# A triangular substitution moved to GpSimd, with a fused state update and fixed priorities, in an RWKV-7 scan

## The chip, the cores and the metric

The kernel runs on one core of a Trainium2 chip. It is one launch; the metric is the device time of that launch in microseconds (us), from its start to its end. The engines named are TensorE (PE, with its weight loads listed apart as PEld), VectorE (DVE), ScalarE (ACT), GpSimd (POOL) and SyncE (SP, which here issues DMA transfers). Each engine works through a queue of its own, in order; between queues, semaphores make an instruction wait for another engine's result.

## The reference, cut to what matters

The reference is one layer of a hybrid encoder: 1024 tokens of 1024 features go through three token mixers (an mLSTM, a long convolution by FFT, and a bidirectional RWKV-7 recurrence), which are gated, projected and merged. The change touches the RWKV-7 recurrence alone. It has 16 heads of 64, and runs once forwards and once backwards over the tokens:

```python
def rwkv7_scan(r, w, k, v, kk, a, reverse):
    def step(state, inp):
        r_t, w_t, k_t, v_t, kk_t, a_t = inp
        sa = jnp.einsum('bhij,bhj->bhi', state, -kk_t)
        state = (state * w_t[:, :, None, :] + sa[..., None] * (kk_t * a_t)[:, :, None, :]
                 + v_t[..., None] * k_t[:, :, None, :])
        return state, jnp.einsum('bhij,bhj->bhi', state, r_t)
    ...
    _, ys = lax.scan(step, jnp.zeros((B, H, N, N), jnp.float32), xs, reverse=reverse)
```

## The kernel before, in words

The launch has four stretches. Until about 865 us come the modulation, the mLSTM and the long convolution; then the preparation of the recurrence's first pair of heads; from 929 to about 1984 us the recurrence over 8 head pairs; then the last norms, the merge and the output projection.

The recurrence is computed in chunks of 64 tokens, 16 chunks a pair, both directions in one go. Inside a chunk the tokens depend on one another through a strictly triangular matrix; its inverse is needed for every chunk and is made ahead of the scan, for eight chunks (one half, g = 0 or 1) at a time, by `tphase`. `tphase` multiplies out the blocks (`pq`, PE), copies them (`quad`, `q21`, ACT), transposes them (`Ab`, DVE, L1625), loads an identity into `Tb` by DMA (L1628), and then solves by substitution: 31 steps, each a product `tm = Ab column x Tb row` and an addition `Tb += tm` (L1630 to L1638; DVE, by the helper at L476). That is 62 instructions that depend on one another, with 16 to 136 elements a partition; it is done 16 times (8 pairs, 2 halves). Two transposes of the result follow (`t1`, L1641, printed as tile `t`, and `t2`, L1644, DVE), then two rounds of small products (`pwx`, PE) and copies into `tt` (ACT). The scan of the chunks of that half reads `tt`.

`scan` runs a chain of links in each chunk m: products U (G by SV, PE); copy `us` out of PSUM (DVE, L1769); products SA (`tt` by `us`, PE); two copies of halves of SA into `SV` (DVE L1775 and ACT L1776); products SN (PE); the new state `sn` = (SN + old state) x `pc`, two DVE instructions (L1787, L1788; helper line L476); two copies of halves of `sn` into the next `SV` (DVE L1800, ACT L1801); the next chunk. The chunk's outputs (`outputs`) are products and copies beside the chain. All tiles U, SA, SN of a chunk lie in one PSUM tile `pch`.

What runs beside the chain: `setup` (the matrices G and B of two chunks), `prep` (decays, keys and so on of the next pair: DVE, ACT, PE), `load`, `post` of the pair before, `bonus`, `tphase` of the next half, and the large products with the input weights (`pg`), which `self.fill` hands out evenly. A weight tile for these is loaded by DMA (`wraw`), cast on ACT (`wh`, L333) and its remainder formed on GpSimd (`wl`, L334); `wl` and `wh` have four buffers each.

The order is set in two ways. `rwkv` has a table of 64 steps a pair, four for each chunk: `put(generator, steps)` says at which steps a generator runs on to its next `yield`, and `weave` goes through the table, filling in products. Then a scheduler of the tile framework, which sees everything that the table has emitted, puts each engine's queue in order by when it expects operands to be ready and by priority: `ahead(tc, ..., TP)` raises `tphase` by 400, `tc.high_priority(10 ** 6)` puts an instruction before all that are ready, and `tc.issue_after(x)` puts it behind x. PSUM tile `banks` ("pq", "pgr", "ptv", "pwx") has one buffer, which these four share.

Of the kernel before, what the change touches and what calls it, by code (L numbers as in the profile page):

```python
# [285 lines left out]
class Trunk:  # L286
# [104 lines left out]
    def in_turn(self, calls, ins=None):  # L391

        for f in calls:
            if ins is None:
                ins = f()  # L395
                continue
            with self.tc.issue_after(ins.ins), self.tc.high_priority(10 ** 6):
                ins = f()  # L398
        return ins

# [946 lines left out]
    def rwkv(self, yc_out, pairs=range(8)):  # L1347
        nc, tc, A = self.nc, self.tc, self.A
        with ExitStack() as c2:
# [39 lines left out]
            n = len(pairs)  # L1389
            cx = [dict(p=p, ar={}, al={}, bk={}, pc={}) for p in pairs]  # L1390
# [10 lines left out]
            for i in range(n):  # L1401
                at = {}

                def put(gen, *steps):
                    for s in steps:
                        at.setdefault(s, []).append(gen)
                put(prep1, 0, 0, 1, 2, 3, 4, 4)
                put(self.bonus(cx[i]), 5, 6, 7)
                put(ahead(tc, self.tphase(cx[i], 1), TP), *range(6, 28, 2))
                if i + 1 < n:  # L1410
# [4 lines left out]
                    put(ahead(tc, self.tphase(nx, 0), TP), *range(39, 62, 2))  # L1415
# [181 lines left out]
    def tphase(self, cx, g):  # L1597
# [3 lines left out]
        nc, rp = self.nc, self.rp  # L1601
# [28 lines left out]
        for l in range(31):  # L1630
            n, m = 31 - l, l // 2 + 1
            x = tm[:, 0:n * m].rearrange("p (a b) -> p a b", b=m)
            self.tt(x, Ab[:, l + 1:32, l].unsqueeze(2).broadcast_to([128, n, m]),
                    Tb[:, l, 0:m].unsqueeze(1).broadcast_to([128, n, m]))
            o = Tb[:, l + 1:32, 0:m]
            self.tt(o, o, x, ADD)
            if l % 5 == 4:
                yield  # L1638
        tt = self.tt_t[g]
        t1 = x2("t1").rearrange("p a b -> p (a b)").rearrange("p (v s) -> p v s", s=16)  # L1640
        nc.vector.transpose(t1.rearrange("p v s -> p s v"), Tb.rearrange("p t s -> p s t"))  # L1641
# [98 lines left out]
    def scan(self, cx, nx):  # L1740
# [13 lines left out]
        for m in range(16):  # L1754
# [14 lines left out]
            nc.vector.tensor_copy(us, U)  # L1769
# [5 lines left out]
            nc.vector.tensor_copy(SV[0:64, 0, both], SA[0:64])  # L1775
            nc.scalar.copy(SV[0:64, 1, both], SA[64:128])  # L1776
# [6 lines left out]
            pc = cx["pc"][g][:, :, c:c + 1].broadcast_to([128, 2, 64])  # L1783
            if m == 0:
                self.tt(S1, SN, pc)
            else:
                self.tt(S1, SN, S0, ADD)  # L1787
                self.tt(S1, S1, pc)  # L1788
# [8 lines left out]
            if m < 15:  # L1797

                SV, at = now[2], now[4]
                nc.vector.tensor_copy(SV[0:64, 0, at], S1[0:64])  # L1800
                nc.scalar.copy(SV[0:64, 1, at], S1[64:128])  # L1801
# [114 lines left out]
```

## Time and profile before

| | us |
|---|---|
| median of 3 runs | 2187.23 (2184.51 to 2191.09) |
| the profiled execution | 2200.05 |
| its span, first to last instruction | 2198.3 |
| first `us` copy of the scan, pair 0 | 929.48 |
| first `us` copy of pair 7 | 1884.68 |
| last `us` copy | 1983.3 |
| mean TensorE clock that the throttle granted | 0.956 of full speed |

The profile has one execution, and all durations come from it; the median comes from runs of their own. A row of a timeline reads: start, duration, engine, source line, operation, output <- inputs, partitions x elements a partition, count, and in brackets how long the engine had been idle and for whom. A row of a group reads: line, engine, operation, output <- inputs, forms, count, then busy time and mean duration in ns, then the idle time before it and what ended that. Helpers record under their own lines: L476 is any DVE two-input operation, L395 and L398 are matmuls that are issued in a fixed turn.

### The profile page before, as it was taken

The page shows a single profiled execution, that of the slowest core. Times are in us where ns is not written, and L with a number is a line of the kernel's source. Part 1 is how long each engine was busy: PE and PEld are TensorE (multiplying, and loading weights), DVE is VectorE, ACT ScalarE, POOL GpSimd, SP SyncE. Part 2 cuts the span into 40 slices and gives each one's busy share as a digit, 9 for nine tenths or more (in the row PEclk, how much of TensorE's full clock was granted, in tenths as well). Part 3 has the DMA queues.
Part 4 walks back from the last instruction along what each step waited for, and adds up shares of the span by engine and source line. Part 5 has one row for each costly group of instructions (what it writes and reads, how often), then busy time and mean ns, then how long its engine had stood idle before and what let it go on. Part 6 is the DMA issues. An engine that isn't in the chain of part 4 may idle for free. (4 is left out here: it accounts for less than half of the span.)

```text
span 2198.3 us, 45984 instructions
## 1 busy us (share of the span) xinstructions
PE 1994.0 (91%) x17098; PEld 1509.2 (69%) x17098; DVE 1634.6 (74%) x4754; ACT 1103.2 (50%) x2558; POOL 424.3 (19%) x485
## 2 busy tenths in 40 slices
PE   6999899999989899899989999999898887897998
PEld 4666777787868677666766676666666665675786
DVE  4854999988447947788787888868887888764536
ACT  5557356454242115664665756667466564532221
POOL 2211311122222432311101111111114411010200
PEclk9999999999999999999998999999899998897999
DMA  8211222334465345321322333224143542445623
GB/s 255 70 67 59 78 77 90 112 101 127 143 200 172 119 138 163 124 68 61 130 79 93 117 106 102 92 81 136 52 155 118 187 144 63 159 143 175 196 89 129
DMA packets 169384, 262.19 MB, mean 119 GB/s; under 512 B 17863, under 2 KB 87335, under 8 KB 169160
## 3 DMA queue, kind: packets, MB, share of 16 engines
q1 hardware_dynamic: 169160, 259.25, 36.3%
q8 instruction: 135, 2.21, 0.4%
q14 instruction: 89, 0.73, 0.1%
HBM read 181.06 MB, written 78.12 MB: 118 GB/s over the span
## 5 line engine op out<-in xcount | busy, mean ns | idle before, releaser
L334 POOL TENSOR_TENSOR wl<-wraw,wh 128x256 fp32r<-128x256 f32 x408 | 371.5, 915 | 1488.6 <-ACT wh L333 1464.8
L351 PE MATMUL pg<-hh,wh 128*128 128x512 f32 x1440 | 601.5, 418 | 20.9 <-ACT wh L333 11.8
L352 PE MATMUL pg<-hh,wl 128*128 128x512 f32 x1440 | 594.3, 413 | 16.4 <-POOL wl L334 16.3
L353 PE MATMUL pg<-hl,wh 128*128 128x512 f32 x1440 | 592.4, 412 | 1.9 <-DVE hl L565 1.8
L351 PEld LDWEIGHTS pg<-hh,wh 128*128 128x128 f32 x1440 | 278.7, 194 | 88.9 <-ACT wh L333 15.1
L352 PEld LDWEIGHTS pg<-hh,wl 128*128 128x128 f32 x1440 | 279.3, 194 | 78.0 <-POOL wl L334 22.2
L353 PEld LDWEIGHTS pg<-hl,wh 128*128 128x128 f32 x1440 | 278.1, 193 | 62.0 <-DVE hl L565 2.8
L333 ACT CAST wh<-wraw 128x256 fp32r<-128x256 f32 x408 | 162.7, 404 | 220.6 <-PE pg L353 122.1
L476 DVE TENSOR_TENSOR tm<-Ab,Tb 128x126 f32<-128x126 f32 (+22 forms) x496 | 145.4, 293 | 4.4 <-DMA Tb<-in_tinit 2.7
L476 DVE TENSOR_TENSOR Tb<-Tb,tm 128x126 f32<-128x126 f32 (+22 forms) x496 | 144.2, 291 | 1.9
L473 DVE SCALAR_TENSOR_TENSOR st<-pg,hmu,st 128x511 f32<-128x511 f32 (+1 forms) x130 | 80.9, 636 | 27.9 <-ACT e L424 17.6
L476 DVE TENSOR_TENSOR G<-pgr,gmask 128x512 f32<-128x512 f32 x128 | 85.4, 679 | 17.0 <-PE pgr L398 17.0
L457 ACT ACTIVATE st<-pg 128x512 f32<-128x512 f32 x74 | 44.2, 597 | 99.9 <-PE pg L353 95.0
L1684 ACT COPY G<-ar 64x128 f32<-64x128 f32 x256 | 64.3, 295 | 48.4 <-DVE G L476 46.6
L473 DVE SCALAR_TENSOR_TENSOR st<-st,pg 128x512 f32<-128x512 f32 x80 | 54.3, 679 | 35.7 <-PE pg L353 12.7
L398 PE MATMUL pgr<-ar,bk 64*128 64x128 f32 x896 | 76.9, 287 | 0.0
L141 DVE SCALAR_TENSOR_TENSOR row<-row 64x1 f32<-64x1 f32 x393 | 72.7, 208 | 2.1
L1769 DVE COPY us<-pch 128x128 f32<-128x128 f32 x128 | 36.3, 283 | 45.8 <-PE pch L398 45.5
L395 PEld LDWEIGHTS pch<-SV,G 128*64 128x64 f32 x256 | 25.3, 139 | 65.5 <-ACT SV L1801 52.3
L395 PE MATMUL pch<-SV,G 128*64 128x64 f32 x256 | 43.2, 252 | 27.7 <-ACT SV L1801 26.2
L476 DVE TENSOR_TENSOR dw<-dw,dw 128x512 f32<-128x512 f32 x92 | 67.1, 760 | 0.9
L395 PEld LDWEIGHTS pch<-SV,B 128*64 128x64 f32 x256 | 25.3, 139 | 60.1 <-ACT SV L1776 50.1
(677 smaller groups left out, 4228.4 us busy)
## 6 DMA issues: line engine op xcount, KB each, us to landing
wraw<-in_w_in SPq DMA_DIRECT2D x340, 128.0 KB, 2.3
low<-lora SPq DMA_DIRECT2D x32, 512.0 KB, 4.1
sig<-st SPq DMA_DIRECT2D x48, 256.0 KB, 2.6
st<-sig SPq DMA_DIRECT2D x48, 256.0 KB, 3.5
wraw<-in_w_br SPq DMA_DIRECT2D x68, 128.0 KB, 2.8
adw<-in_ada_w SPq DMA_DIRECT2D x16, 512.0 KB, 7.1
x<-in_x SPq DMA_DIRECT2D x8, 512.0 KB, 6.1
hx<-st SPq DMA_DIRECT2D x16, 256.0 KB, 2.0
```

Of the source, the lines that this page charges most:

```text
L141: self.ops.append(lambda: self.nc.vector.scalar_tensor_tensor(o, a, s, b, op0=op0, op1=op1))
L333: self.nc.scalar.copy(hi, raw)
L334: self.nc.gpsimd.tensor_tensor(lo, raw, hi.bitcast(F32), op=SUB)
L351: nc.tensor.matmul(p, wh, hh, start=(k == 0), stop=False)
L352: nc.tensor.matmul(p, wl, hh, start=False, stop=False)
L353: nc.tensor.matmul(p, wh, hl, start=False, stop=(k == n - 1))
L395: ins = f()
L398: ins = f()
L457: self.nc.scalar.activation(o, p, AF.Tanh, scale=0.5)
L473: return self.nc.vector.scalar_tensor_tensor(out, in0, s, in1, op0=op0, op1=op1)
L476: return self.nc.vector.tensor_tensor(out, a, b, op=op)
L1684: nc.scalar.copy(G[0:64, :, d, h, 0:64], cx["al"][g, d, b % 4][hsl[h]])
```

## The change

Three things change. The 62 instructions of a substitution are issued on GpSimd instead of DVE; the table gives `tphase` other steps, with one more `yield` ahead of the transposes, and transpose `t1` is to be issued behind the latest `us` copy that has been emitted (`self.mark`). The state update for m > 0 becomes one multiply-add from PSUM for each direction, `sn` = SN x `pc` + `sd`, where `sd` is the old state times `pc`, which ACT has made a chunk ahead. And `us`, the copies into `SV` and `sn` get the highest priority (`first`).

```diff
--- before.py
+++ after.py
@@ -397,6 +397,10 @@
             with self.tc.issue_after(ins.ins), self.tc.high_priority(10 ** 6):
                 ins = f()
         return ins
+
+    def first(self):
+
+        return self.tc.high_priority(10 ** 6)
 
     def banks(self, name):
 
@@ -1387,6 +1391,7 @@
 
             pairs = list(pairs)
             n = len(pairs)
+            self.mark = None
             cx = [dict(p=p, ar={}, al={}, bk={}, pc={}) for p in pairs]
             run(self.load(cx[0]))
             for g in range(2):
@@ -1406,13 +1411,13 @@
                         at.setdefault(s, []).append(gen)
                 put(prep1, 0, 0, 1, 2, 3, 4, 4)
                 put(self.bonus(cx[i]), 5, 6, 7)
-                put(ahead(tc, self.tphase(cx[i], 1), TP), *range(6, 28, 2))
+                put(ahead(tc, self.tphase(cx[i], 1), TP), 6, *range(7, 14), 24, 26, 28)
                 if i + 1 < n:
                     nx = cx[i + 1]
                     put(self.load(nx, cx[i - 1] if i else None), 8, 9, 10, 11)
                     put(ahead(tc, self.prep(nx, 0, 0), PP), 15, 16, 19, 33, 33)
                     put(ahead(tc, self.prep(nx, 0, 1), PP), 34, 35, 36, 37, 37)
-                    put(ahead(tc, self.tphase(nx, 0), TP), *range(39, 62, 2))
+                    put(ahead(tc, self.tphase(nx, 0), TP), 39, *range(40, 47), 57, 59, 61)
                     prep1 = ahead(tc, chain(self.prep(nx, 1, 0), self.prep(nx, 1, 1)), PP)
                     put(prep1, 40, 42, 49)
                 if i > 0:
@@ -1598,7 +1603,7 @@
 
 
 
-        nc, rp = self.nc, self.rp
+        nc, tc, rp = self.nc, self.tc, self.rp
         x2 = lambda n: self.ep.tile([128, 16, 32], F32, name=n, tag="x2", bufs=3)
         q, q21 = x2("quad"), self.ep.tile([128, 16, 32], F32, name="q21", tag="q21", bufs=1)
         pq = [x.rearrange("p (c t) -> p c t", t=CL) for x in self.banks("pq")]
@@ -1630,15 +1635,18 @@
         for l in range(31):
             n, m = 31 - l, l // 2 + 1
             x = tm[:, 0:n * m].rearrange("p (a b) -> p a b", b=m)
-            self.tt(x, Ab[:, l + 1:32, l].unsqueeze(2).broadcast_to([128, n, m]),
-                    Tb[:, l, 0:m].unsqueeze(1).broadcast_to([128, n, m]))
+            nc.gpsimd.tensor_tensor(x, Ab[:, l + 1:32, l].unsqueeze(2).broadcast_to([128, n, m]),
+                                    Tb[:, l, 0:m].unsqueeze(1).broadcast_to([128, n, m]), op=MUL)
             o = Tb[:, l + 1:32, 0:m]
-            self.tt(o, o, x, ADD)
+            nc.gpsimd.tensor_tensor(o, o, x, op=ADD)
             if l % 5 == 4:
                 yield
+        yield
         tt = self.tt_t[g]
         t1 = x2("t1").rearrange("p a b -> p (a b)").rearrange("p (v s) -> p v s", s=16)
-        nc.vector.transpose(t1.rearrange("p v s -> p s v"), Tb.rearrange("p t s -> p s t"))
+
+        with tc.issue_after(self.mark.ins) if self.mark else ExitStack():
+            nc.vector.transpose(t1.rearrange("p v s -> p s v"), Tb.rearrange("p t s -> p s t"))
         t1 = t1.rearrange("p (g u) s -> p u s g", g=2)
         t2 = x2("t2")
         nc.vector.transpose(t2.rearrange("p u (s g) -> p u s g", g=2), t1)
@@ -1766,26 +1774,35 @@
             if late:
                 late[0](ins)
             us = self.sm.tile([128, 2, CL], F32, name="us", tag="us", bufs=2)
-            nc.vector.tensor_copy(us, U)
+            with self.first():
+                self.mark = nc.vector.tensor_copy(us, U)
             ins = self.in_turn(partial(nc.tensor.matmul, SA[hsl[h], d], tt[hsl[h], 8 * d + c, :], us[hsl[h], d],
                                        start=True, stop=True) for d in range(2) for h in range(2))
             if late:
                 late[1](ins)
             late = None
-            nc.vector.tensor_copy(SV[0:64, 0, both], SA[0:64])
-            nc.scalar.copy(SV[0:64, 1, both], SA[64:128])
+            with self.first():
+                nc.vector.tensor_copy(SV[0:64, 0, both], SA[0:64])
+                nc.scalar.copy(SV[0:64, 1, both], SA[64:128])
             yield
             next(ahead, None)
             yield
             self.in_turn(partial(nc.tensor.matmul, SN[hsl[h], d], B[:, j, d, hsl[h]], SV[:, h, at[d]],
                                  start=True, stop=True) for d in range(2) for h in (1, 0))
             S1 = self.sm.tile([128, 2, 64], F32, name="sn", tag="sn", bufs=3)
-            pc = cx["pc"][g][:, :, c:c + 1].broadcast_to([128, 2, 64])
-            if m == 0:
-                self.tt(S1, SN, pc)
-            else:
-                self.tt(S1, SN, S0, ADD)
-                self.tt(S1, S1, pc)
+            pc = cx["pc"][g][:, :, c:c + 1]
+            with self.first():
+                if m == 0:
+                    self.tt(S1, SN, pc.broadcast_to([128, 2, 64]))
+                else:
+                    for d in range(2):
+                        self.stt(S1[:, d], SN[:, d], pc[:, d], S0d[:, d])
+            if m < 15:
+
+                S0d = rp.tile([128, 2, 64], F32, name="sd", tag="sd", bufs=2)
+                pc = cx["pc"][(m + 1) // 8][:, :, (m + 1) % 8:(m + 1) % 8 + 1]
+                for d in range(2):
+                    nc.scalar.activation(S0d[:, d], S1[:, d], AF.Copy, scale=pc[:, d])
             late = self.outputs(y, py, m, S0, ar, now)
             S0 = S1
             if m < 15:
@@ -1797,8 +1814,9 @@
             if m < 15:
 
                 SV, at = now[2], now[4]
-                nc.vector.tensor_copy(SV[0:64, 0, at], S1[0:64])
-                nc.scalar.copy(SV[0:64, 1, at], S1[64:128])
+                with self.first():
+                    nc.vector.tensor_copy(SV[0:64, 0, at], S1[0:64])
+                    nc.scalar.copy(SV[0:64, 1, at], S1[64:128])
             yield
             next(ahead, None)
             yield
```

The first place is DVE's queue where the substitution for the fourth `tphase` ends. `Tb`, `tm`, `Ab` are the substitution, `bk`, `ar`, `P`, `s`, `st` work of `prep` and of the weight products, `us`, `SV`, `sn` links of the chain; `t_` and a number is `t1` or `t2`. Before:

```order
L476 TENSOR_TENSOR Tb<-Tb,tm 128x3x15
L476 TENSOR_TENSOR ar<-r,P 128x4x64
L476 TENSOR_TENSOR tm<-Ab,Tb 128x30
L476 TENSOR_TENSOR bk<-tmp,s 128x4x64
L476 TENSOR_TENSOR Tb<-Tb,tm 128x2x15
L1769 COPY us<-pch 128x128
L476 TENSOR_TENSOR tm<-Ab,Tb 128x16
L476 TENSOR_TENSOR bk<-a,s 128x4x64
L476 TENSOR_TENSOR Tb<-Tb,tm 128x16
L1641 STREAM_TRANSPOSE t_11650<-Tb 128x16x32
```

After, with the line numbers of the changed file (`us` is L1778 there, `SV` L1785 and L1818, `t1` L1649, `t2` L1652):

```order
L477 SCALAR_TENSOR_TENSOR P<-P,hlgb,tmp 128x512
L477 SCALAR_TENSOR_TENSOR s<-s,hlgb,a 128x512
L477 SCALAR_TENSOR_TENSOR sn<-pch,pc,sd 128x64 x2
L477 SCALAR_TENSOR_TENSOR st<-st,pg 128x512
L1818 COPY SV<-sn 64x2x64
L477 SCALAR_TENSOR_TENSOR P<-P,hlgb,tmp 128x512
L1778 COPY us<-pch 128x128
L1649 STREAM_TRANSPOSE t_11757<-Tb 128x16x32
L1785 COPY SV<-pch 64x2x64
L1652 STREAM_TRANSPOSE t_11759<-t_11757 128x512
L477 SCALAR_TENSOR_TENSOR s<-s,hlgb,a 128x512
L480 TENSOR_TENSOR P<-P,tmp 128x512
```

The substitution is gone from this queue. `t1` stands directly behind a `us` copy, and the `SV` copy of the same chunk directly behind `t1`.

The second place is GpSimd's queue, first before, from the weights' remainders of one pair to the next:

```order
L334 TENSOR_TENSOR wl<-wraw,wh 128x256 x14
L1555 MEMSET s 128x8
L334 TENSOR_TENSOR wl<-wraw,wh 128x256 x3
L1555 MEMSET s 128x8 x2
L334 TENSOR_TENSOR wl<-wraw,wh 128x256
L1555 MEMSET s 128x8
L334 TENSOR_TENSOR wl<-wraw,wh 128x256 x3
L1699 MEMSET SV 64x512
```

After, at the end of one substitution and the beginning of the next (L1638 is the product, L1641 the addition, L1560 and L1707 are the memsets that were L1555 and L1699):

```order
L1641 TENSOR_TENSOR Tb<-Tb,tm 128x2x15
L1638 TENSOR_TENSOR tm<-Ab,Tb 128x16
L1641 TENSOR_TENSOR Tb<-Tb,tm 128x16
L334 TENSOR_TENSOR wl<-wraw,wh 128x256 x4
L1560 MEMSET s 128x8
L334 TENSOR_TENSOR wl<-wraw,wh 128x256
L1560 MEMSET s 128x8
L334 TENSOR_TENSOR wl<-wraw,wh 128x256 x2
L1560 MEMSET s 128x8
L1707 MEMSET SV 64x512
L1638 TENSOR_TENSOR tm<-Ab,Tb 128x31
L1641 TENSOR_TENSOR Tb<-Tb,tm 128x31
```

Between two substitutions stand the remainders `wl` and memsets; within a substitution each instruction waits for the one ahead of it, and one to four `wl` are interspersed.

## The prediction

> **What bounds the kernel now.** The share of busy time comes first, then the waits, then windows, since the scan's eight head pairs have stages with different limits.
>
> ```profile
> PE 1994.0 (91%) x17098; PEld 1509.2 (69%) x17098; DVE 1634.6 (74%) x4754; ACT 1103.2 (50%) x2558; POOL 424.3 (19%) x485
> ...
> 929.48 0.29 DVE L1769 COPY us<-pch 128x128 f32<-128x128 f32 x1 [2.31 <-PE pch L398]
> ...
> 1884.68 0.29 DVE L1769 COPY us<-pch 128x128 f32<-128x128 f32 x1 [1.71 <-PE pch L398]
> ```
>
> These are each engine's busy time, and the first copy `us` of pair 0 and of pair 7 (start, length, wait before it in brackets). Seven pairs take 955.2 us, 136.46 us a pair, 8.5 us for each of 16 chunks. PE's 91% has modelled ends, so it is no proof that PE sets the pace. The waits between 929 and 1984 us (total, times, longest) show that the scan's own links are waited for:
>
> ```profile
> POOL wl L334 <- ACT wh L333: 753.2, 132, 39.2
> ACT SV L1801 <- DVE sn L476: 55.4, 39, 4.9
> PEld pch L395 <- ACT SV L1801: 52.3, 71, 5.8
> PEld pch L395 <- ACT SV L1776: 49.6, 81, 2.2
> ACT SV L1776 <- DVE SV L1775: 48.7, 44, 3.9
> DVE us L1769 <- PE pch L398: 45.5, 45, 3.5
> ```
>
> GpSimd idles most, for weights that ACT casts. PE and ACT wait for links that pass through DVE. Where DVE makes them late, windows of pair 2 show (start:end, length, busy time of PE, PEld, DVE, ACT, POOL with instructions, granted clock, DMA share, GB/s):
>
> ```profile
> 1193.34:1207.59 14.25, 12.97 (x235) 9.90 (x237) 10.12 (x20) 11.88 (x29) 1.46 (x2) 1.00 0.34 113
> 1207.59:1246.36 38.77, 35.04 (x322) 25.44 (x318) 35.21 (x115) 23.77 (x60) 6.33 (x8) 1.00 0.41 135
> 1246.36:1270.97 24.61, 23.59 (x465) 17.75 (x464) 19.13 (x41) 21.68 (x52) 1.89 (x4) 1.00 0.30 91
> 1270.97:1306.53 35.56, 33.95 (x333) 24.15 (x331) 32.88 (x127) 16.37 (x42) 6.02 (x8) 1.00 0.20 64
> 1306.53:1323.29 16.76, 16.55 (x241) 12.22 (x243) 8.20 (x20) 11.35 (x22) 0.73 (x1) 1.00 0.43 152
> ```
>
> The second and fourth are the substitutions, from the end of transpose `Ab` to transpose `t1`. There DVE is busy for 35.21 of 38.77 and 32.88 of 35.56 us, 92%: it is full. Elsewhere it is busy for 37.45 of 55.62 us, 67%. The same two windows with `tm` and `Tb` alone (DVE):
>
> ```profile
> 1207.59:1246.36 38.77, 17.46 (x62) 1.00 0.41 135
> 1270.97:1306.53 35.56, 16.64 (x62) 1.00 0.20 64
> ```
>
> So 17.05 us of DVE per substitution, half of its work there, leaves it; 17.0 us stay (17.75 and 16.24). Fifteen such windows lie in the scan. The ends of the first and the last:
>
> ```profile
> 944.07 1.95 DVE L1625 STREAM_TRANSPOSE Ab<-quad 128x1024 f32<-128x1024 f32 x1 [0.39 <-ACT quad L1620]
> 977.89 1.09 DVE L1641 STREAM_TRANSPOSE t<-Tb 128x512 f32<-128x512 f32 x1
> ...
> 1895.73 1.98 DVE L1625 STREAM_TRANSPOSE Ab<-quad 128x1024 f32<-128x1024 f32 x1
> 1937.46 1.10 DVE L1641 STREAM_TRANSPOSE t<-Tb 128x512 f32<-128x512 f32 x1
> ```
>
> The first is 977.89 − 946.02 = 31.9 us, the last 39.8. The 14 of pairs 0 to 6 sum to 541.5, 38.7 each. A pair is thus 2 × 38.7 = 77.4 us of windows and 59.1 us of the rest.
>
> **The substitution on GpSimd.** No row shows `tm` or `Tb` on GpSimd, so T, one substitution there, is built from what it did run:
>
> ```profile
> 198.12 0.73 POOL L334 TENSOR_TENSOR wl<-wraw,wh 128x256 fp32r<-128x256 f32 x1 [1.06 <-DVE row L141]
> 198.87 0.95 POOL L671 MEMSET rm<- 64x1024 f32 x1
> 199.88 0.11 POOL L672 MEMSET rm<- 64x8 f32 x1
> ...
> L930 POOL TENSOR_TENSOR dml<-dw,dmh x4: 1276/1283/1287, 516.7 to 520.4; 128x512 fp32r<-128x512 f32 x4
> ```
>
> A two-input instruction takes 0.73 us for 256 elements a partition and 1.283 for 512: 2.16 ns an element, 0.177 us fixed. Between two GpSimd instructions in a row lie 199.88 − 199.82 = 0.06 us. In step l the loop handles (31 − l)(l // 2 + 1) elements, 2856 in all, twice (multiply and add). T alone = 62 × (0.177 + 0.06) + 2 × 2856 × 0.00216 = 14.7 + 12.3 = 27.0 us.
>
> The Trainium skill, GPSIMD Engine Reference, section "3. Performance versus the Vector engine", measures a GpSimd tensor_tensor at 1.96 times the Vector engine's; 1.96 × 17.05 would make T 33.4 where the sum here comes to 35.6, a total some 33 us lower. The rows agree only roughly: 1.283 us for 512 elements stands beside DVE's 0.68 (1.9 times).
>
> To 27.0 come two things. First, the engines block each other:
>
> ```profile
> 1223.98 1.14 POOL L334 TENSOR_TENSOR wl<-wraw,wh 128x256 fp32r<-128x256 f32 x1 [2.50 <-ACT wh L333]
> 1224.43 0.83 DVE L476 TENSOR_TENSOR tm<-Ab,Tb 128x126 f32<-128x126 f32 x1
> 1225.73 0.28 DVE L476 TENSOR_TENSOR tm<-Ab,Tb 128x136 f32<-128x136 f32 x1
> ...
> 757.60 17.06 POOL L334 TENSOR_TENSOR wl<-wraw,wh 128x256 fp32r<-128x256 f32 x2 [4.18 <-ACT wh L333]
> 763.67 3.69 DVE L476 TENSOR_TENSOR dw<-dw,dw 128x512 f32<-128x512 f32 x6
> 768.01 0.80 PE L352 MATMUL pg<-hh,wl 128*128 128x512 f32 x1 [6.62 <-POOL wl L334]
> ```
>
> A DVE `tm` beside a `wl` took 0.83 instead of 0.28 us, the `wl` 1.14 instead of 0.73; under a run of `dw` multiplies, each with two inputs in SBUF, two `wl` took 17.06 us. Of DVE's other work in a window, what reads two SBUF tiles (as the `bk` and `P` rows below) comes to about 9.2 us by my count of what the changed order puts beside a substitution, at the times of before. Bounds are 0 and all 17.0; I take 0.7 of 9.2, 6.4 us, because DVE has gaps now that half its work is gone. Second, `wl` stands in the same queue:
>
> ```profile
> L334 POOL TENSOR_TENSOR wl<-wraw,wh 128x256 fp32r<-128x256 f32 x165 | 140.4, 854 | 773.2 <-ACT wh L333 753.2 <-PE ptv L1693 11.3 <-issue 4.5
> ```
>
> In this stretch one `wl` takes 0.85 us, and the order puts 2.6 into a substitution: 2.2 us. Its wait for `wh`, 753.2 / 132 = 5.7 us on average, now holds up the substitution if it falls inside; bounds 0 and 5.7, I take 0, as ACT casts ahead while GpSimd is late. What waits for a `wl` behind substitution steps is PE, in order, with the scan's matmuls after it; the last row above shows 6.62 us of that. Four `wl` buffers are the cover, since PE's products use older ones meanwhile; I take 0, and without the cover it is up to 6.62 us a window. **T = 27.0 + 6.4 + 2.2 = 35.6 us**, with bounds 27.0 and 51.9 (27.0 + 17.0 + 2.2 + 5.7).
>
> **The transposes held back.** `t1` stands right behind a `us` copy, four chunks after the substitution's start. DVE runs in order: if `Tb` isn't ready, `t1` stops it, and behind `t1` stands the `SV` copy of the running chunk, for which SN, hence the scan, waits. So a window now lasts at least T, with 0.5 us for the handing over there and back (bounds 0 and 1). With DVE's 17.0 us it could be far shorter: T decides.
>
> **Multiply-add and decay.** The pieces in the scan (count, busy, mean ns):
>
> ```profile
> L476 DVE TENSOR_TENSOR sn<-sn,pc 128x128 f32<-128x128 f32 x119 | 37.0, 311 | 0.6
> L476 DVE TENSOR_TENSOR sn<-pch,sn 128x128 f32<-128x128 f32 x119 | 33.7, 283 | 38.4 <-PE pch L398 32.0 <-ACT st L457 5.0 <-ACT wh L333 0.8
> L476 DVE TENSOR_TENSOR bk<-a,s 128x256 f32<-128x256 f32 x56 | 25.7, 461 | 0.1
> L476 DVE TENSOR_TENSOR y<-y,pch 128x64 f32<-128x64 f32 x124 | 24.1, 209 | 6.2 <-PE pch L398 6.0
> L473 DVE SCALAR_TENSOR_TENSOR P<-P,hlgb,tmp 128x512 f32<-128x512 f32 x14 | 10.9, 780 | 1.9 <-DMA tmp<-z2d 1.1 <-DMA tmp<-z6d 0.6
> L1735 ACT COPY y<-pch 128x64 f32<-128x64 f32 x128 | 21.0, 214 | 36.3 <-PE pch L398 35.5
> ```
>
> Out go 0.311 + 0.283 = 0.594 us a chunk, in come two of 128x64 at 0.209: 0.2 us less. Outside the windows (8 of 16 chunks) that is worth 1.6 us a pair; inside, T covers it. ACT gets 2 × 0.214 = 0.43 us a chunk, 6.9 us a pair. It is hidden, as the decayed state is needed a chunk later and the `SV` copies go ahead of it; uncovered it would cost 6.9 × 8 = 55 us, which is also its bound. Below nothing is excluded: ACT had no such work before.
>
> **The scan's copies first.** This changes DVE's and ACT's order only. Its bounds are from −45.5 us (all of DVE's idle time before `us`) to +10 (other work pushed back); I take 0, since in the windows T sets the pace. The prologue's first substitution lies in a stretch that has
>
> ```profile
> 800.00:929.00 129.00, 119.59 (x801) 94.34 (x799) 96.47 (x187) 66.52 (x127) 33.20 (x34) 1.00 0.49 160
> ```
>
> DVE loses 17 us there and GpSimd gains 27, beside PE's weight products: −17 to +10, taken as 0. Of those products 82 move from ahead of the first chunk to later; PE has to run them anyway.
>
> **The sum.** A pair becomes 59.1 + 2 × 35.6 + 2 × 0.5 − 1.6 = 129.7 us, 6.8 less. Fifteen windows are 7.5 pairs: −51 us. The profiled execution took 2200.05 us (span 2198.3), so 2149; it lies 0.6% above the median of the runs, 2187.23, so × 0.9942: **2136 us**. T may be 39.0 before nothing is left of the gain; the margin is 3.4 us in 35.6.
>
> **The rivals.** *No wait left:* neither blocking nor handing over costs anything, and T is 27.0 + 2.2 = 29.2. A pair is 59.1 + 58.4 − 1.6 = 115.9, −154 us: 2046, × 0.9942 = 2034. For it speaks DVE's 17.0 us in such a window, against it the 1.14 us `wl`. Chance 0.14.
>
> *The substitution becomes the bound (slower):* DVE stands behind `t1`, and the scan with it. All 9.2 us of blocking and one wait for `wh` inside the queue give T = 27.0 + 9.2 + 2.2 + 5.7 = 44.1, a pair of 147.7, +84 us: 2284, × 0.9942 = 2271. It decides from T = 39.0 on. For it speaks the row 757.60, where GpSimd starved under DVE, and that T is extrapolated from two shapes to instructions with broadcast and strided inputs; against it, that DVE's long runs are now broken by waits. Chance 0.32.
>
> On the blocking the Trainium skill, SBUF — State Buffer, section "SBUF: two separate sides", says that whichever engine starts first has the port pair for the whole instruction; GpSimd would then wait for one DVE instruction at a time. The row 757.60 disagrees: there it was held through a run of them.
>
> *It doesn't do what it says:* something else (PE's products, ACT) sets the pace, and the window stays near 38.7 whatever DVE sheds: within 0.3%, 2187. PE's 91% speaks for it, DVE's 92% against 67% speaks against. Chance 0.06.
>
> **How the numbers follow.** The forecast, 2136, has 0.48, with its own range of 2070 to 2170 (T from 31 to 38). Faster by over 0.3%, about what a measurement can tell from no change: 0.48 + 0.14 = 0.62; within 0.3%: 0.06; slower: 0.32. The range reaches from 2045, near the first rival, to 2235, where T is 42 (a pair 3 × 2 = 6 us over before); beyond these I leave 0.2.
>
> **What would show it.** `tm` and `Tb` on GpSimd, in rows: the smallest at 0.21 us and the largest (136 elements) at 0.47; first `tm` to last `Tb` 35.6 us; DVE's idle time before `t1`, put down to GpSimd, as the sign that T sets the window; windows of some 36 us with DVE busy for half of them; `sn` in two rows of 0.2 us. I am wrong if T is over 39, if the windows are shorter than 33, or if the rest of a pair is not 59 us.

## The result and the profile after

The changed kernel takes 2331.81 us (median of 4 runs, 2326.25 to 2347.33) where the kernel before takes 2185.87 on the same chip: a ratio of 1.068, with a 95% interval of 1.062 to 1.074. It is slower by 146 us. The forecast was 2136, the range ended at 2235. The profiled execution took 2326.25 us, 126 more than the one of before.

The page's busy line of the changed kernel, and its groups that answer to those shown of before (count, busy us, mean ns, idle time before them and its releaser):

```profile
PE 2022.0 (87%) x17098; PEld 1517.9 (65%) x17098; DVE 1437.9 (62%) x3762; ACT 1164.5 (50%) x2796; POOL 821.6 (35%) x1477
...
L352 PE MATMUL pg<-hh,wl 128*128 128x512 f32 x1440 | 603.8, 419 | 105.5 <-POOL wl L334 105.2
...
L1638 POOL TENSOR_TENSOR tm<-Ab,Tb 128x126 f32<-128x126 f32 (+22 forms) x496 | 205.4, 414 | 128.2 <-DMA Tb<-in_tinit 60.3
L1641 POOL TENSOR_TENSOR Tb<-Tb,tm 128x126 f32<-128x126 f32 (+22 forms) x496 | 215.2, 434 | 36.4
...
L477 DVE SCALAR_TENSOR_TENSOR sn<-pch,pc,sd 128x64 f32<-128x64 f32 x240 | 56.5, 276 | 85.6 <-PE pch L398 77.6
L1805 ACT ACTIVATE sd<-sn,pc 128x64 f32<-128x64 f32 x240 | 77.8, 344 | 58.1 <-DVE sn L477 55.3
```

DVE shed what it was to shed (74% to 62%), yet the span grew. The substitution itself is as short as forecast: (205.4 + 215.2) / 16 = 26.3 us of instructions, and with the 36.4 us of gaps ahead of `Tb` and as much ahead of `tm` some 31 us. From the first `tm` to the last `Tb`, with the `wl` between, the fifteen of the scan average 33.2 us; T was forecast at 35.6.

The first `us` copies of pair 0 and pair 7, and the last of all (timeline of the changed kernel, DVE):

```profile
910.04 0.29 DVE L1778 COPY us<-pch 128x128 f32<-128x128 f32 x1 [0.36 <-PE pch L398]
...
1977.46 0.29 DVE L1778 COPY us<-pch 128x128 f32<-128x128 f32 x1 [1.61 <-PE pch L398]
...
2106.48 0.29 DVE L1778 COPY us<-pch 128x128 f32<-128x128 f32 x1 [1.25 <-PE pch L398]
```

Seven pairs take 1067.4 us, 152.5 a pair instead of 136.5: 112.2 us more. The scan starts 19.4 us earlier, the last pair takes 129.0 us instead of 98.6, and what follows the scan 2.9 us more, which makes up the 126 us. The 14 windows of pairs 0 to 6 from `Ab` to `t1` last 41.4 us on average instead of 38.7, and the rest of a pair 69.8 instead of 59.1. The waits in the scan (910 to 2107 us; total, times, longest) say who is late:

```profile
DVE us L1778 <- PE pch L398: 175.6, 78, 15.6
...
PEld pg L352 <- POOL wl L334: 92.6, 18, 12.0
PE pg L352 <- POOL wl L334: 86.6, 17, 11.6
...
POOL tm L1638 <- DMA Tb<-in_tinit: 60.3, 5, 23.2
...
PE plw L1557 <- DMA low<-lora: 30.9, 8, 13.5
```

PE and its weight loads wait for `wl` (two views of the same 17 or 18 stalls, some 90 us); before, only the weight loads wait for `wl`, 1.0 us in the scan. DVE's wait for PE rises from 45.5 to 175.6 us. DVE's wait at `t1` for the substitution, which the slower rival rested on, is small (the transposes' own rows: idle until then, us, times):

```profile
L1649 DVE STREAM_TRANSPOSE t<-Tb x16: 1055/1088/1121, 886.2 to 2048.5; 128x512 f32<-128x512 f32 x16
...
  POOL Tb L1641: 23.4, 4
```

One stall of pair 2 shows the path. GpSimd, PE, SP's queue and DVE in the changed kernel's timeline, one fence for each:

```profile
1217.74 0.25 POOL L1638 TENSOR_TENSOR tm<-Ab,Tb 128x31 f32<-128x31 f32 x1 [4.96 <-DMA Tb<-in_tinit]
...
1246.74 0.72 POOL L334 TENSOR_TENSOR wl<-wraw,wh 128x256 fp32r<-128x256 f32 x1
...
1249.79 0.22 POOL L1641 TENSOR_TENSOR Tb<-Tb,tm 128x16 f32<-128x16 f32 x1
1249.97 2.08 POOL L334 TENSOR_TENSOR wl<-wraw,wh 128x256 fp32r<-128x256 f32 x3
```

```profile
1247.51 0.80 PE L352 MATMUL pg<-hh,wl 128*128 128x512 f32 x1 [7.20 <-POOL wl L334]
1256.53 0.79 PE L1557 MATMUL plw<-low,w2h 128*128 128x512 f32 x1 [7.36 <-DMA low<-lora]
```

```profile
1226.13 0.32 SPq L1484 DMA_DIRECT2D bon<-mm  x1
1247.49 4.24 SPq L330 DMA_DIRECT2D wraw<-in_w_in  x3
1251.82 0.38 SPq L1552 DMA_DIRECT2D low<-lora  x1
```

```profile
1259.70 0.29 DVE L1778 COPY us<-pch 128x128 f32<-128x128 f32 x1 [15.63 <-PE pch L398]
...
1267.82 1.08 DVE L1649 STREAM_TRANSPOSE t<-Tb 128x512 f32<-128x512 f32 x1
```

No `wl` was formed from 1217.7 to 1246.7. PE stood 7.2 us for it with the chain's products behind. SP stood from 1226.5 to 1247.5 at a `wraw` load, whose buffer came free with the late `wl`; behind it stood `low`, for which PE then waited 7.4 us more. The chunk's `us` copy waited 15.6 us, and the substitution, done at 1250.0, lay ready for 17.8 us until `t1`.

### The profile page after: what moved, and what is told of

Same layout as the page of the kernel before. It is cut to its first block, busy times and chain, and to the rows that moved or that the text cites. A ratio compares the mean times of both kernels' runs of the same rounds, so it can differ in the third digit from the quotient of the medians.

```text
span 2324.4 us, 46267 instructions
## 1 busy us (share of the span) xinstructions
PE 2022.0 (87%) x17098; PEld 1517.9 (65%) x17098; DVE 1437.9 (62%) x3762; ACT 1164.5 (50%) x2796; POOL 821.6 (35%) x1477
## 4 chain that ended last, share of the span: by engine, by line
PE 40%; POOL 20%; DVE 12%; issue 11%; DMA 8%; ACT 8%; SPq 1%; POOLq 0%; DVEq 0%; ACTq 0%
POOL Tb L1641 8%; POOL tm L1638 8%; PE pg L351 8%; PE pg L352 7%; PE pg L353 7%; PE pout L1263 4%; POOL wl L334 3%; PE pch L398 2%; PE pch L395 2%; DMA wraw<-in_w_in 1%; PE pG L957 1%; DVE st L477 1%; DVE dw L480 1%; DMA low<-lora 1%; PE pwx L398 1%
## 5 line engine op out<-in xcount | busy, mean ns | idle before, releaser
L334 POOL TENSOR_TENSOR wl<-wraw,wh 128x256 fp32r<-128x256 f32 x408 | 354.1, 874 | 1064.3 <-ACT wh L333 1036.5
L352 PE MATMUL pg<-hh,wl 128*128 128x512 f32 x1440 | 603.8, 419 | 105.5 <-POOL wl L334 105.2
L351 PE MATMUL pg<-hh,wh 128*128 128x512 f32 x1440 | 618.9, 430 | 20.7 <-ACT wh L333 13.3
L1638 POOL TENSOR_TENSOR tm<-Ab,Tb 128x126 f32<-128x126 f32 (+22 forms) x496 | 205.4, 414 | 128.2 <-DMA Tb<-in_tinit 60.3
L1641 POOL TENSOR_TENSOR Tb<-Tb,tm 128x126 f32<-128x126 f32 (+22 forms) x496 | 215.2, 434 | 36.4
L1778 DVE COPY us<-pch 128x128 f32<-128x128 f32 x128 | 36.8, 288 | 176.1 <-PE pch L398 175.6
L477 DVE SCALAR_TENSOR_TENSOR sn<-pch,pc,sd 128x64 f32<-128x64 f32 x240 | 56.5, 276 | 85.6 <-PE pch L398 77.6
L1805 ACT ACTIVATE sd<-sn,pc 128x64 f32<-128x64 f32 x240 | 77.8, 344 | 58.1 <-DVE sn L477 55.3
L480 DVE TENSOR_TENSOR G<-pgr,gmask 128x512 f32<-128x512 f32 x128 | 86.0, 678 | 29.5 <-PE pgr L398 29.5
L461 ACT ACTIVATE st<-pg 128x512 f32<-128x512 f32 x74 | 44.1, 596 | 103.5 <-PE pg L353 98.6
L395 PEld LDWEIGHTS pch<-SV,G 128*64 128x64 f32 x256 | 25.3, 139 | 74.8 <-ACT SV L1819 49.4
```

What stands on the lines that cost most here:

```text
L334: self.nc.gpsimd.tensor_tensor(lo, raw, hi.bitcast(F32), op=SUB)
L351: nc.tensor.matmul(p, wh, hh, start=(k == 0), stop=False)
L352: nc.tensor.matmul(p, wl, hh, start=False, stop=False)
L477: return self.nc.vector.scalar_tensor_tensor(out, in0, s, in1, op0=op0, op1=op1)
L480: return self.nc.vector.tensor_tensor(out, a, b, op=op)
L1638: nc.gpsimd.tensor_tensor(x, Ab[:, l + 1:32, l].unsqueeze(2).broadcast_to([128, n, m]), Tb[:, l, 0:m].unsqueeze(1).broadcast_to([128, n, m ...
```

## The experiments

The theories. **Q** (queue): `wl` stands behind the substitution on GpSimd. **T** (length): the substitution is too long there, and DVE stands at `t1`. **R** (rest): table, state update or priorities cost the time; in its parts **D** (decay on ACT) and **P** (priorities). All ratios are to the kernel before on the same chip, with 95% intervals.

| kernel | us | ratio | interval |
|---|---|---|---|
| the change | 2331.81 | 1.068 | 1.062 to 1.074 |
| gpsimd_alone | 2404.43 | 1.102 | 1.096 to 1.108 |
| gpsimd_table | 2328.84 | 1.065 | 1.061 to 1.069 |
| no_first | 2317.66 | 1.061 | 1.056 to 1.066 |
| raw7 | 2323.22 | 1.063 | 1.058 to 1.067 |
| wh_twice | 2317.80 | 1.063 | 1.060 to 1.065 |
| wl_on_vector | 2231.05 | 1.021 | 1.015 to 1.027 |
| no_wl | 2219.65 | 1.016 | 1.012 to 1.021 |
| wl_on_vector_no_first | 2206.60 | 1.008 | 1.005 to 1.012 |
| wl_on_vector_sub_only | 2191.42 | 1.004 | 1.001 to 1.007 |
| sub_on_vector | 2218.72 | 1.015 | 1.011 to 1.020 |
| table_alone | 2179.61 | 0.998 | 0.995 to 1.001 |
| state_alone | 2216.51 | 1.014 | 1.009 to 1.018 |
| order_alone | 2236.22 | 1.023 | 1.018 to 1.028 |
| state_and_order | 2276.18 | 1.041 | 1.036 to 1.047 |
| short_sub | 2123.46 | 0.973 | 0.972 to 0.975 |
| less_pe | 2212.81 | 1.014 | 1.012 to 1.016 |

### Which part costs: the substitution, its table, or the rest

sub_on_vector takes the changed kernel and puts the substitution back:

```diff
-            nc.gpsimd.tensor_tensor(x, ..., op=MUL)
+            self.tt(x, ...)
-            nc.gpsimd.tensor_tensor(o, o, x, op=ADD)
+            self.tt(o, o, x, ADD)
```

> The changed kernel with the 62 instructions of a substitution back on DVE; table, transposes behind `us`, multiply-add, decay on ACT and priorities stay. Theory Q (queue: on GpSimd the substitution stands ahead of the weights' remainders `wl`; PE, in order, waits for them, and SP's queue behind the `wraw` loads, whose buffers `wl` frees): PE's wait for `wl` in the scan falls from some 87 us to under 10, and the time to 2160 to 2210. Theory T (length: the substitution itself is too long on GpSimd, so DVE waits behind `t1`): the same fall. Theory R (rest: the table, the decay on ACT or the priorities cost the time): it stays above 2270.

2219: most of the loss is the substitution's (PE's products wait for `wl` only 3.4 us), but 1.5% stays, just beyond the 2160 to 2210 that Q and T both expected, so this run does not part them. gpsimd_alone is the reverse edit of the kernel before, with its old table:

> The kernel before with the substitution's instructions on GpSimd and nothing else changed (old table, no hold on the transposes, old state update, no priorities). Theory Q: the loss is there in full, 2300 to 2360, with PE waiting for `wl` for 70 us or more. Theory T: also slower, but by DVE's wait at `t1`, and more than the changed kernel, as nothing holds `t1` back: above 2360. Theory R: within 2180 to 2250.

2404, as T expected (above 2360) and not Q: with nothing to hold `t1` back, DVE stands there, and PE's products wait for `wl` only 11.1 us. DVE's waits (903 to 2180 us):

```profile
DVE t L1641 <- POOL Tb L1636: 248.6, 14, 19.7
DVE us L1769 <- PE pch L398: 85.9, 75, 3.4
```

So theory T holds for the old table, and the new table with its hold does what it was made for: 248.6 us of this wait became 23.4 in the changed kernel. gpsimd_table adds table and hold to gpsimd_alone (the changed kernel with the old `sn` lines, and without `first`):

> Part one of the change alone: substitution on GpSimd with the new table and the hold on the transposes; old state update, no priorities. The substitution alone with the old table took 10% more than before, the whole change 6.8%, the state and the priorities on their own 1.4% and 2.3%. Theory Q (PE waits for `wl` behind the substitution; this is nearly all of the loss): 2290 to 2330, with PE's wait for `wl` at 80 us or more. If instead the parts' costs add up: 2333 - 2183 x 3.6% = 2230 to 2270.

2329, as Q expected: nearly the whole loss is there, and state and priorities add nothing that can be told from none to it (1.065 against 1.068, intervals overlapping). The parts don't add up. no_first tests the same from the other side:

```diff
     def first(self):
-        return self.tc.high_priority(10 ** 6)
+        return ExitStack()
```

> The changed kernel without the priorities (table, hold, GpSimd and state as changed). With the substitution on GpSimd nothing of it stands behind the chain on DVE. Theory P in its wider form (priorities cost anywhere): 2240 to 2290. Theory P as bound to a substitution on DVE: the priorities do no harm here, and the time stays at 2310 to 2350, as the wait for `wl` stays.

2318: the priorities aren't what is slow here. table_alone is the kernel before with the table and the hold:

> The kernel before with the new table and the hold on the transposes alone; substitution on DVE, old state update, no priorities. With state and priorities this took 2219, 1.5% over before. If those cost their 1.4% and 2.3% here too, the table gains 2%: 2125 to 2155. If the table is neutral and the priorities cost less with it: 2170 to 2200.

2180: no difference that can be measured. The table is neutral by itself.

### Is it the queue behind the substitution?

wl_on_vector moves the `wl` of the recurrence's stretch (180 of the kernel's 408) off GpSimd:

```diff
-        self.nc.gpsimd.tensor_tensor(lo, raw, hi.bitcast(F32), op=SUB)
+        (self.nc.vector if self.scanning else self.nc.gpsimd).tensor_tensor(lo, raw, hi.bitcast(F32), op=SUB)
```

> The changed kernel with the `wl` of the recurrence's stretch (some 140 instructions) on DVE, so that nothing but the substitution and a few memsets stands in GpSimd's queue. Theory Q: PE's wait for `wl` falls from some 87 us to under 20 and SP's wait at the `wraw` loads to under half; the time falls by 90 to 150 us, to 2180 to 2240, less what 140 x 0.4 us cost on DVE. Theory T: the windows still last as long as the substitution, and the time stays above 2300. Theory R: above 2300.

2231: 101 us come back, as Q expected and T and R excluded, though DVE now has these instructions too. SP's wait at `wraw` fell from 441.2 us (put down to `wl`) to 241.9, slightly above the half that was expected. Before it is 350.6 us, so SP's standing there is not a loss by itself: it costs where something behind it, such as `low`, comes late.

wh_twice was to part PE's wait for `wl` from SP's:

```diff
-            nc.tensor.matmul(p, wl, hh, start=False, stop=False)
+            nc.tensor.matmul(p, wh if self.scanning else wl, hh, start=False, stop=False)
```

> The changed kernel, where the second of the three weight products in the recurrence's stretch multiplies by `wh` again instead of by `wl`: PE has the same work but never waits for `wl` there, while GpSimd still forms `wl` behind the substitution, and SP's `wraw` loads still wait for it. (The input products of that stretch lack their `wl` part.) If PE's own wait is nearly all of the loss: 2190 to 2240, as with `wl` on DVE (2231). If SP's queue is half of it: 2265 to 2300.

2318: neither. PE needs no `wl` in the scan any more, and almost nothing came back. PE's large waits in that trace are these (timeline, PE; first the stall of pair 2 that was shown above):

```profile
1256.17 0.79 PE L1561 MATMUL plw<-low,w2h 128*128 128x512 f32 x1 [16.60 <-DMA low<-lora]
```

```profile
1177.04 0.40 ACT L335 CAST wh<-wraw 128x256 fp32r<-128x256 f32 x1 [11.86 <-DMA wraw<-in_w_in]
```

```profile
1178.07 0.37 PE L397 MATMUL pch<-SV,G 128*64 128x64 f32 x1 [11.55 <-ACT SV L1823]
```

PE reached the missing `low` earlier and waited longer, to the same moment (1256.2 against 1256.5). At another place ACT stood 11.9 us at the cast of a weight that SP had not loaded, and the `SV` copy of the chain stood behind that cast. The late `wl` thus holds the scan by three doors: PE's product, SP's queue, and ACT's queue. Shutting one leaves the others. raw7 tried the second door, with seven `wraw` buffers:

```diff
+        self.loads += 1
+        rp, nr = (self.rp, 4) if self.scanning and self.loads % 7 > 2 else (self.wp, 3)
```

> The changed kernel with seven buffers for `wraw` in the recurrence's stretch instead of three, `wl` still on GpSimd. It parts theory Q's two waits: SP no longer stands at a `wraw` load, so what lies behind it on SP's queue (`low`, `Tb`'s identity, `bon`) comes in time, while PE's wait for `wl` stays. If SP's queue is half of the loss: 2240 to 2290, with PE's wait for `low` from 31 to under 10 us and GpSimd's for `Tb`'s identity from 60 to under 15. If PE's wait for `wl` is nearly all: 2295 to 2335.

2323, in the range of the case that PE's wait is nearly all, but it settles nothing about the split: SP still waited 399.3 us for `wl` at the `wraw` loads, and PE's wait for `low` stayed at 30.4 us. That agrees with loads that only ran further ahead into the same jam. no_wl opens all doors at once, on top of wh_twice:

```diff
+        if self.scanning:
+            return [(hi[:, j, :], hi[:, j, :]) for j in range(2)]
```

> As wh_twice (the second weight product of the recurrence's stretch multiplies by `wh`, so that the input products there lack their `wl` part), and the `wl` instructions of that stretch aren't issued at all: GpSimd has only the substitution and memsets there, and a `wraw` buffer is free when ACT has cast it. If `wl` behind the substitution is the one cause, with several doors: 2190 to 2230, near the 2231 of the changed kernel with `wl` on DVE, and SP's waits at `wraw` fall to under 150 us. If the substitution on GpSimd costs by itself: above 2280.

2220, within what Q expected. The substitution is on GpSimd as in the changed kernel; the only instructions that are gone against wh_twice are the `wl`, and 98 us go with them. (SP's wait at `wraw` stayed at 283.4 us, not under 150, but now for ACT's casts.) So Q is shown in this form: the loss is there when substitution and `wl` are both on GpSimd, and most of it goes when either leaves (sub_on_vector, 2219; no_wl, 2220). No run took `wl` away with the substitution on DVE, so what that alone would bring isn't measured.

The substitution's length isn't without effect. With `wl` out of its way DVE does stand at `t1` for it (wl_on_vector, then no_wl; DVE, in the scan):

```profile
DVE t L1653 <- POOL Tb L1645: 52.4, 12, 9.1
```

```profile
DVE t L1655 <- POOL Tb L1647: 37.9, 9, 7.2
```

In the changed kernel `Tb` lay ready ahead of `t1` in 12 of the 16 substitutions; the other four make up the 23.4 us.

wl_on_vector_no_first and wl_on_vector_sub_only take the priorities, then also the new state update out of wl_on_vector:

> The changed kernel with `wl` on DVE and without the priorities, the new state update kept. If the priorities cost with the substitution off DVE: 2190 to 2215. If the decay on ACT costs alone: 2220 to 2240.

> The same (substitution on GpSimd, new table, hold; old state update, no priorities), with the `wl` of the recurrence's stretch on DVE. Theory Q, with the rest of 2231 (the changed kernel with `wl` on DVE) put down to state and priorities: 2150 to 2195. If GpSimd's length is what is left of the loss: 2215 to 2250, with DVE's wait at `t1` for GpSimd at 50 us or more as there.

2207 and 2191, both in the ranges that put the rest down to priorities and state: with the queue clear the priorities cost 1.3% and the state update 0.5%, though the last isn't clear of the noise (intervals overlapping). What is left of the change, the substitution on GpSimd with `wl` on DVE, is 0.4% slower than before. The expected gain isn't there even then.

### What state update and priorities cost with the substitution on DVE

state_and_order, state_alone and order_alone are the kernel before with both, with `sd` alone, and with `first` alone:

> The kernel before with the multiply-add on the state decayed by ACT and the priorities alone; substitution on DVE with the old table. Theories Q and T: 2150 to 2190, as the pieces come to -1.6 us a pair outside the windows and 0.2 us a chunk inside them. Theory R in the form that the decay or the priorities cost: above 2230.

> The kernel before with the multiply-add and the decay on ACT alone (no priorities, old table, substitution on DVE). The kernel with state and priorities together takes 2276, 4.1% over before. Theory D (decay: two instructions of 0.345 us a chunk on ACT, with SV copies and casts behind them, hold up the chain): 2240 to 2290. Theory P (priorities: the chain's copies go ahead of the substitution on DVE, which then isn't done when the scan reaches the other half): 2165 to 2195, within 0.5% of before.

> The kernel before with the priorities on `us`, the `SV` copies and `sn` alone (old state update in two DVE steps, old table, substitution on DVE). Theory P: 2250 to 2290, with chunks 7 and 15 of a pair at about 30 us as in the kernel with both. Theory D: within 0.7% of before.

2276, 2217 and 2236. The first is above 2230, as R expected; Q and T had expected 2150 to 2190. D and P each expected that the other part costs nothing, and both were wrong; neither kernel reached the range of its own theory. Each part costs, 1.4% and 2.3%, and together 4.1%. Without priorities the decay stands ahead of the chain's copy on ACT (state_alone, timeline):

```profile
1208.43 0.59 ACT L1804 ACTIVATE sd<-sn,pc 128x64 f32<-128x64 f32 x2
1209.03 0.30 ACT L1818 COPY SV<-sn 64x128 f32<-64x128 f32 x1
```

That puts 0.59 us into a link, and so it is at all 120 of these copies. With priorities the chain runs ahead of its own preparation. The end of the first half of pair 0 in state_and_order (windows: chunks 1 to 6, then chunk 7; all engines, then DVE's `tm` and `Tb` alone):

```profile
924.94:958.09 33.15, 31.92 (x468) 23.11 (x463) 26.82 (x90) 24.35 (x76) 3.09 (x6) 1.00 0.20 60
958.09:987.56 29.47, 27.97 (x285) 21.40 (x280) 20.04 (x52) 15.16 (x38) 4.48 (x6) 0.94 0.27 88
```

```profile
924.94:958.09 33.15, 10.15 (x38) 1.00 0.20 60
958.09:987.56 29.47, 6.99 (x24) 0.94 0.27 88
```

Six chunks take 33.2 us, 5.5 each, and the next one 29.5: in it DVE does the last 24 instructions of the substitution that the following half needs. The other pairs show the same: from `us` copy to `us` copy, chunks 7 and 15 last 29.7 and 31.8 us on average, 25.3 and 26.2 in order_alone, and 10.8 and 15.5 before. This agrees with copies put first starving the preparation of the next half; no run tried the substitution at the same priority.

### Did DVE set the pace before?

short_sub leaves out 50 of a substitution's 62 instructions in the kernel before (25 of 31 steps, so that the inverse is incomplete), less_pe the second weight product in the recurrence's stretch:

```diff
-        for l in range(31):
+        for l in (4, 9, 14, 19, 24, 29):
```

> The kernel before with 6 of the 31 steps of each substitution (50 of 62 instructions left out, some 13.7 us of DVE a substitution, 206 us in the fifteen of the scan), all else as before. If DVE sets the pace in those windows, as the prediction's first step has it: 120 to 200 us less, 1985 to 2065. If PE, 90% busy throughout, sets it: at most 60 us less, 2125 to 2183.

```diff
-            nc.tensor.matmul(p, wl, hh, start=False, stop=False)
+            if not self.scanning:
+                nc.tensor.matmul(p, wl, hh, start=False, stop=False)
```

> The kernel before without the second of the three weight products in the recurrence's stretch (the `wl` part, some 560 matmuls of 0.39 us or more, 218 us of PE); `wl` is still formed, all else as before. If PE sets the pace: 150 to 220 us less, 1965 to 2035. If DVE does: at most 60 us less, 2125 to 2183. If both share it (one in the substitution's windows, the other outside): 70 to 140 less.

2123: taking some 206 us off DVE in the scan, for nothing, brings 59 us. That is what the case "PE sets it" allowed at most, and less than half of the least that "DVE sets it" expected. Where the time went, the first `us` copies of pair 0 and pair 7 and the ends of pair 0's window show (short_sub, timeline, DVE):

```profile
894.34 0.29 DVE L1769 COPY us<-pch 128x128 f32<-128x128 f32 x1 [0.40 <-PE pch L398]
...
965.84 1.92 DVE L1625 STREAM_TRANSPOSE Ab<-quad 128x1024 f32<-128x1024 f32 x1 [0.32 <-ACT quad L1620]
976.63 1.10 DVE L1641 STREAM_TRANSPOSE t<-Tb 128x512 f32<-128x512 f32 x1
...
1796.43 0.29 DVE L1769 COPY us<-pch 128x128 f32<-128x128 f32 x1 [0.70 <-PE pch L398]
```

This window lasts 8.9 us, and the 14 of pairs 0 to 6 average 8.1 instead of 38.7. But a pair still takes 128.9 us instead of 136.5: the rest of it grew from 59.1 to 112.6. DVE's wait for PE ahead of `us` rose from 45.5 to 84.5 us.

But less_pe, with some 218 us less for PE to do, is slower, 2213, outside all its ranges. It can't be read as PE's share, because the granted clock fell. Three stretches of the scan, first before, then less_pe (the clock is the third number from the end):

```profile
929.00:1250.00 321.00, 295.63 (x3748) 218.88 (x3748) 257.21 (x777) 190.35 (x482) 43.15 (x58) 0.95 0.29 93
1250.00:1600.00 350.00, 324.36 (x4174) 238.31 (x4173) 281.07 (x841) 217.34 (x530) 44.99 (x62) 0.98 0.29 96
1600.00:1984.00 384.00, 335.42 (x4220) 245.65 (x4217) 305.33 (x840) 216.08 (x541) 81.52 (x95) 0.93 0.42 134
```

```profile
929.00:1250.00 321.00, 288.81 (x3669) 211.73 (x3668) 262.66 (x779) 198.55 (x501) 56.72 (x77) 0.96 0.33 110
1250.00:1600.00 350.00, 276.60 (x3719) 205.73 (x3717) 280.79 (x813) 213.87 (x520) 61.67 (x81) 0.84 0.31 99
1600.00:1984.00 384.00, 300.26 (x3999) 228.06 (x4001) 280.21 (x831) 199.59 (x503) 38.36 (x52) 0.78 0.35 115
```

PE's busy time in them fell by 90 us, not by 218. One pair is worth a look, pair 3, first before, then less_pe:

```profile
1323.29:1459.52 136.23, 127.53 (x1603) 93.32 (x1601) 109.76 (x329) 83.16 (x207) 22.11 (x28) 1.00 0.31 101
```

```profile
1329.92:1465.45 135.53, 96.60 (x1376) 73.83 (x1377) 102.77 (x321) 75.76 (x182) 3.16 (x8) 0.69 0.24 78
```

There PE ran 26 weight products instead of 257 and was busy for 31 us less, and the pair was as long as before. That the lower clock stretched the chain's own products instead isn't excluded.

## Why the prediction was wrong

**Length of the substitution:** right. T was forecast at 35.6 us and measured 33.2; the smallest and largest instructions, forecast at 0.21 and 0.47 us, took 0.22 and 0.53 to 0.57. A price taken from 256 and 512 elements held roughly for 16 to 136; of the 6.4 us put in for blocking some 3 came. By the ratio of 1.96 to DVE that the Trainium skill, GPSIMD Engine Reference, "3. Performance versus the Vector engine", measures at 2048 elements, the instructions would have taken 33.4 us, an estimate. They took 26.3, 1.5 times DVE's 17.05, and the measurement decides.

**What waits behind it in GpSimd's queue:** this step failed. The prediction named the danger and priced it: "Four `wl` buffers are the cover, since PE's products use older ones meanwhile; I take 0, and without the cover it is up to 6.62 us a window." The cover was too thin: one weight tile of eight blocks takes all four buffers, and in the stall shown no new `wl` was formed for 29 us. Clearing the queue brought back 112 us in no_wl, 7.5 us for each of the fifteen windows, and from gpsimd_table to wl_on_vector_sub_only 137 us, 9.2 a window. So even the bound of 6.62 lay below the value. It was also too narrow in kind: it counted PE's wait, while SP's and ACT's queues stood too, so that removing PE's wait alone (wh_twice) gave back 14 us of 146, which the intervals can't tell from nothing. Of the 196 us between forecast and result, by no_wl, 112 are this queue, 51 the gain that isn't there, and some 34 what no_wl still takes beyond the kernel before.

**The transposes held back:** the hold worked (248.6 to 23.4 us at `t1`). The slower rival, DVE standing there once T exceeds 39, was the wrong mechanism for the right sign: T is 33, and `Tb` lay ready before `t1` while PE was late. Where DVE does stand there, in wl_on_vector and no_wl, T is 33 and 32 as well, and the windows last 35.2 and 33.8 us, less than the 38.7 of before: that wait alone makes no window longer.

**State update:** mis-sized. It was to save 0.2 us a chunk on DVE. A multiply-add of 128x64 takes 0.276 us, not the 0.209 of the row used for it, so the two take 0.55 where 0.59 were removed, and ACT's part is 0.69 us a chunk, not 0.43. Alone it costs 1.4%. There `sd` runs ahead of the `SV` copy all 120 times; the prediction, which had the priorities in mind, put it behind and took it as hidden.

**Priorities:** taken as 0, at most +10 us; they cost 2.3% alone (53 us) and 1.3% with the queue clear, but nothing that shows while `wl` holds up the scan.

**What bounds the kernel:** this step failed too. DVE is 92% busy in the substitution's windows, and the prediction took it that a pair gets shorter by what a window loses, with the rest of it staying at 59.1 us. The rest does not stay. In short_sub the windows lose 30.6 us each and the rest gains 53.5; in no_wl the windows came out much as forecast, 33.8 us, but the rest is 70.2, and a pair takes 137.8 us instead of 136.5. In the changed kernel itself the rest is 69.8: the prediction's own sign of being wrong. So little was to be had from the start: leaving out four fifths of the substitution gives 59 us in all, where the same reading (13.7 us in each of 15 windows) gives 206 and the forecast gain was 51 for moving it. Whether PE or the chain's own latency takes over when DVE is relieved stays open, as less_pe changed the clock along with the work.

**Start and end of the scan:** the prologue was taken as 0, and the last pair was to gain half of what the others gain. The first `us` copy came 19.4 us earlier, but the last pair took 30.4 us more. In no_wl too it takes 123.5 us instead of 98.6; why stays open.

No kernel tried here that does the whole work beats the one before by more than can be measured; table_alone (0.998, interval 0.995 to 1.001) comes nearest.

## What to carry to other kernels

Before moving a long chain of dependent instructions to an idle engine, list what else is in that engine's queue and follow each such instruction to its reader and to the buffer that it frees: here a chain of 33 us held back 0.72 us instructions by up to 29 us, and a buffer that came free late stopped the queues of other engines. If such a wait is to be called covered, count the buffers against the chain's length. And a busy share of 92% in a window does not say that the whole gets shorter by what is taken out: here the window shrank and the rest of the pair grew. Leave the work out once, and see what that is worth at most.

## What the runs showed of the hardware

Less work for TensorE went with a lower granted clock: 0.96, 0.84 and 0.78 in three stretches of less_pe, where before has 0.95, 0.98 and 0.93; in the stalled stretch of the changed kernel from 1216 to 1268 us it was 0.77:

```profile
1216.30:1267.82 51.52, 36.49 (x293) 25.42 (x293) 23.06 (x52) 24.69 (x63) 29.61 (x66) 0.77 0.27 89
```

The products behind the two stalls in it start every 0.42 to 0.43 us, those ahead of them every 0.23 (timeline, PE):

```profile
1231.60 0.39 PE L353 MATMUL pg<-hl,wh 128*128 128x512 f32 x1
1231.83 0.39 PE L351 MATMUL pg<-hh,wh 128*128 128x512 f32 x1
...
1257.54 0.63 PE L352 MATMUL pg<-hh,wl 128*128 128x512 f32 x1
1257.97 0.63 PE L353 MATMUL pg<-hl,wh 128*128 128x512 f32 x1
1258.40 0.63 PE L351 MATMUL pg<-hh,wh 128*128 128x512 f32 x1
```

So a stall of PE costs a little beyond its own length: for the same 17098 products PE was busy 2022.0 us instead of 1994.0. The Trainium skill, TensorE: Matmul & The Clock Gate, section "Part 1: The HAM clock gate (the "warmup" mystery)", has the clock halved after about 3.4 us of idleness. Two stalls of over 7 us, and products that start at little more than half the rate behind them, agree with that.

And GpSimd and DVE disturbed one another less than feared: the 62 instructions took 26.3 us on GpSimd beside DVE's work, 3 more than 62 x 0.177 + 2 x 2856 x 0.00216 = 23.3, which is what the prediction's prices give without any blocking. That DVE's instructions had gaps between them now, as the prediction argued, fits this, but no run shows it to be the reason.
